# An NSA + HGRN2 decoder trunk on one core: the first HGRN projection pair, the order of the last two units, and where row-major weights lie

## The chip, the cores and the metric

The kernel runs on one of the eight cores of a Trainium2 chip. A core has TensorE (PE in the rows: matmuls; PEld: its weight loads), VectorE (DVE), ScalarE (ACT), GpSimd (POOL) and SyncE (SP), an on-chip memory of 128 partitions (SBUF), and a small accumulator memory that matmuls write (PSUM). Transfers between HBM and SBUF are DMAs; here SP issues those of weights and results, POOL those of the residual stream. The metric is the device time of one execution in microseconds (us), lower is better; several executions give a median.

## The reference, cut to what matters

The input is x, 512 tokens by 2048 features, float32. Two layers are computed, then a final RMSNorm:

```python
for layer in range(2):
    hn = rmsnorm(x, norm_w[layer])
    y = nsa_mixer(hn, ...) if layer == 0 else hgrn2_mixer(hn, ...)
    x = x + y
return rmsnorm(x, final_norm_w)
```

`nsa_mixer` is attention with compressed, selected and windowed keys over 16 heads of 128; its output is gated by silu(z) and projected by `w_out`. `hgrn2_mixer` is a gated linear recurrence:

```python
q, f, i, z = split(hn @ w_in)                   # 16 heads of 128 each
k = (1 - lb) * sigmoid(-f); q = silu(q)          # and the decay from f
o = recurrence over 512 tokens of (q, k, i, decay), per head
o = rmsnorm(o) * gnorm_w * silu(z); y = o @ w_out
```

So every HGRN head needs four projected inputs: F and Q (which give its decay, keys and queries), I (its values) and Z (its gate). All weights are float32 and are read once from HBM.

## The kernel before, in words

**Precision.** Each float32 operand is split into a rounded part `hi` (a ScalarE cast to fp32r) and the rest `lo` (a VectorE subtraction), `split`, L76 to L80. A product is three matmuls: hi·hi, hi·lo and lo·hi. The normalised stream lies in SBUF as `hhi` and `hlo`, 128 features by 512 tokens for each of 16 feature blocks (kt). Each weight load of 512 KB lands in a `raw` buffer and is split into two or four tiles `whi`/`wlo` of 512 floats per partition (tags `whi`, `wlo`, `ohi`, `olo`, four buffers each).

**NSA layer** (`nsa`, L649). Heads are worked in groups; at its end `out_proj_half` (L291) projects heads 12 to 15, tokens in two halves: first tiles 0 and 1, then tiles 2 and 3 of 128 tokens. After each half the sum x is written to a DRAM tile `xd` (POOL, L730) and `norm(1, t)` (L474) makes the new `hhi`/`hlo` of those tokens: square sums, a scale `xn` on ACT or DVE, four PE transposes for each 512 features, `y` on DVE, then the split. The pools of this layer have three raw buffers.

**HGRN layer** (`hgrn`, L912). It opens its own pools in the SBUF space that the NSA pools leave: level tiles (attT 2 x 2048 bytes, pick 3 x 512, masks 6 x 64 bytes per partition), a spacer `GAP` of 48 floats, then the weight tiles, work tiles and five raw buffers. In the NSA layer what lies in front of the weight tiles is causal, cmask, rt, kcmp, vcmp, gate and sw, 9,984 bytes. A tile of a new pool waits until the old tiles under it are done with.

The first unit there is head 0's F and Q, by `proj_pair` (L116): both weights are loaded and split whole, F into `whi`/`wlo`, Q into `ohi`/`olo`, and the tokens are taken in two halves of 256; each half is 48 matmuls for F and 48 for Q. All other F/Q pairs and the Z pairs go through `proj_product` (L168), which takes half of the contraction as seven products of 2 x 2 blocks (Strassen-like, over the sums `fm` made once by `forms`, L135) and the other half (`rest`) directly. A helper tile `s2` of 256 floats holds a partial sum. Its fifth product is the last reader of `fm` in a pair and stands between `rest(a)` and `rest(b)`.

I units go through `proj_rows` (L238): here the weights are the moving operand (256 columns, two heads at once) and `hhi`/`hlo` the stationary one, 192 matmuls for two heads. `hgrn_levels` computes from F and Q the within-chunk attention `attT`; `hgrn_inner` (L1099) needs `attT` and I; `hgrn_gate` needs Z.

**Order around the change.** The loop (L928) takes heads two at a time: levels of both, I of both, Z of both. While it runs, x lives in `xd`, and the SBUF place of x holds `fm`. The last two heads are written out: levels, I (L940), Z (L941), then `open_x` (L943) puts x back over `fm`, sixteen POOL loads of 256 KB (L947) fetch it, then `hgrn_inner` of both, the gates, `out_proj` of heads 12 and 13 (which adds to x in SBUF, L289) and `last_out_proj` of heads 14 and 15 (L510), whose four weight loads (L517) are split into the space of `hhi`/`hlo` blocks 0 to 7.

**Who sets the order.** The program order above is not the issue order: the framework simulates a time line while it builds, and interleaves instructions on each engine as they become ready there. On the chip each engine then runs its own list in order.

Of the kernel before, what the change touches and what calls it, by code (L numbers as in the profile page):

```python
# [52 lines left out]
class Trunk:  # L53
    def __init__(self, ctx, tc, aps):
        self.tc, self.nc, self.ctx = tc, tc.nc, ctx
        self.__dict__.update(aps)
        pool = lambda name, bufs, **k: ctx.enter_context(tc.tile_pool(name=name, bufs=bufs, **k))
        self.consts = pool("consts", 1)
        self.work = pool("work", 2)
        self.spill = pool("spill", 1, space=bass.MemoryType.DRAM).tile([S, D], F32, name="xd")  # L60
        self.pproj = pool("pproj", 2, space=PSUM)
        self.flip = 0
        self.ss = {}
        self.og, self.z = {}, {}
        self.spilled, self.atright = False, None


    def copy(self, out, in_):
# [15 lines left out]
        self.nc.sync.dma_start(raw, ap)  # L84
        return self.split_weights(raw, tags, share)

    def split_weights(self, raw, tags=("whi", "wlo"), share=False):

        _, nk, cols = raw.shape
        parts, step = [], 512 // cols  # L90
        for k0 in range(0, nk, step):
            n = min(step, nk - k0)
            hi, lo = (self.wpool.tile([128, n, cols], F32R, name=t, tag=t, bufs=4) for t in tags)
            self.split(raw[:, k0:k0 + n, :], hi, lo, share and k0)
            parts += [(hi[:, k, :], lo[:, k, :]) for k in range(n)]
        return parts
# [71 lines left out]
    def proj_product(self, w, ca, cb):  # L168


        nc = self.nc
        add = lambda o, a, b: nc.vector.tensor_tensor(out=o, in0=a, in1=b, op=ALU.add)
        raws = []
        for c0 in (ca, cb):
            raw = self.rawpool.tile([128, 2 * KP, 128], F32, name="raw", tag="raw")
            nc.sync.dma_start(raw, w[:2 * KP * 128, c0:c0 + 128].rearrange("(k p) n -> p k n", p=128))
            raws.append((raw[:, :KP], raw[:, KP:]))
        (b11, b21), (b12, b22) = raws

        def parts(src):  # L180
            hi, lo = (self.wpool.tile([128, KP, 128], F32R, name=t, tag=t, bufs=4) for t in ("whi", "wlo"))
            self.split(src, hi, lo)
            return hi, lo

        def product(dst, form, wts, start=False, stop=False):
            (hi, lo), (fhi, flo) = wts, self.fm[form]
            for k in range(KP):
                nc.tensor.matmul(dst, hi[:, k], fhi[:, k], start=start and k == 0, stop=False)
                nc.tensor.matmul(dst, hi[:, k], flo[:, k], start=False, stop=False)
                nc.tensor.matmul(dst, lo[:, k], fhi[:, k], start=False, stop=stop and k == KP - 1)  # L190

        def rest(acc, c0):
            src = w[2 * KP * 128:, c0:c0 + 128].rearrange("(k p) n -> p k n", p=128)
            for k, (hi, lo) in enumerate(self.load_split(src, [128, KT - 2 * KP, 128])):
                kt = 2 * KP + k
                for ts in (one, two):
                    stop = kt == KT - 1 and ts is two
                    nc.tensor.matmul(acc[:, ts], hi, self.hhi[:, kt, ts], start=False, stop=False)  # L198
                    nc.tensor.matmul(acc[:, ts], hi, self.hlo[:, kt, ts], start=False, stop=False)  # L199
                    nc.tensor.matmul(acc[:, ts], lo, self.hhi[:, kt, ts], start=False, stop=stop)  # L200

        one, two = slice(0, 256), slice(256, 512)
        a = self.pproj.tile([128, S], F32, name="acc", tag="acc")
        b = self.pproj.tile([128, S], F32, name="acc", tag="acc")
        d = self.pd.tile([128, S], F32, name="d", tag="d")
        sa, sb = (self.hp.tile([128, S], F32, name=n, tag=n, bufs=1) for n in ("sa", "sb"))
        s2 = self.hp.tile([128, 256], F32, name="s2", tag="s2", bufs=1)
        w2, w1 = parts(b21), parts(b11)
        product(a[:, one], 2, w2, start=True)
        product(d[:, two], 1, w1, start=True, stop=True)  # L210
        nc.scalar.copy(sa[:, one], d[:, two])
        t1, t3 = b11, b12
        add(t1, b11, b12)
        add(t3, b12, b22)
        w7 = parts(t3)
        product(d[:, one], 7, w7, start=True, stop=True)
        w3 = parts(b22)
        product(b[:, one], 3, w3, start=True)
        t2, t4 = b22, b21
        add(t2, t1, b22)  # L220
        add(t4, t2, b21)
        w4 = parts(t4)
        product(a[:, two], 4, w4)
        w6 = parts(t2)
        product(d[:, two], 6, w6, start=True, stop=True)
        add(s2, d[:, two], sa[:, one])
        add(sa[:, two], d[:, one], s2)
        rest(a, ca)
        add(sa, a, sa)
        w5 = parts(t1)  # L230
        product(d[:, two], 5, w5, start=True, stop=True)
        add(sb[:, one], d[:, two], s2)
        add(sb[:, two], d[:, one], sb[:, one])
        rest(b, cb)
        nc.vector.tensor_tensor(out=sb, in0=b, in1=sb, op=ALU.subtract)
        return sa, sb

    def proj_rows(self, w, c0, c1):  # L238
# [3 lines left out]
        for c in range(2):  # L242
            parts = []
            for r0 in range(c * 1024, (c + 1) * 1024, 512):
                raw = self.rawpool.tile([128, 4, 2, 128], F32, name="raw", tag="raw")
                if c1 == c0 + 128:
                    src = w[r0:r0 + 512, c0:c0 + 256].rearrange("(k p) (b n) -> p k b n", p=128, b=2)
                    self.nc.sync.dma_start(raw, src)
                else:
                    for b, cb in enumerate((c0, c1)):  # L250
                        self.nc.sync.dma_start(raw[:, :, b, :],
                                               w[r0:r0 + 512, cb:cb + 128].rearrange("(k p) n -> p k n", p=128))
                parts += self.split_weights(raw.rearrange("p k b n -> p k (b n)"))
            for i, acc in enumerate(accs):
                for k, (hi, lo) in enumerate(parts):
                    kt = c * 8 + k
                    first, last = kt == 0, kt == KT - 1
                    for t in range(2):
                        ts = slice((2 * i + t) * 128, (2 * i + t + 1) * 128)
                        self.nc.tensor.matmul(acc[:, t, :], self.hhi[:, kt, ts], hi, start=first and t == 0, stop=False)  # L260
                        self.nc.tensor.matmul(acc[:, t, :], self.hhi[:, kt, ts], lo, start=False, stop=False)  # L261
                        self.nc.tensor.matmul(acc[:, t, :], self.hlo[:, kt, ts], hi, start=False, stop=last and t == 1)  # L262
# [356 lines left out]
    def gates(self, w_in):  # L619
# [5 lines left out]
        for c in range(2):  # L625
            raw = self.rawpool.tile([128, 8, n], F32, name="raw", tag="raw")
            nc.sync.dma_start(raw, w_in[c * 1024:(c + 1) * 1024, NSA_GL:NSA_Z].rearrange("(k p) n -> p k n", p=128))
            for k0 in (0, 4):
                w = self.wpool.tile([128, 4, 128], F32R, name="whi", tag="whi", bufs=4)
                self.split(raw[:, k0:k0 + 4, :], w[:, :, :n], w[:, :, n:2 * n])  # L630
                for k in range(4):
                    kt = c * 8 + k0 + k
# [16 lines left out]
    def nsa(self):  # L649
# [28 lines left out]
        with ExitStack() as es:  # L678
# [48 lines left out]
            for tiles in ((0, 1), (2, 3)):  # L727
                self.out_proj_half(w_out, 12, last, tiles, self.square_sum)
                for t in tiles:
                    nc.gpsimd.dma_start(self.spill[t * 128:(t + 1) * 128, :], self.x_sb[t])  # L730
                    self.norm(1, t, pool=self.att)

    def query(self, w_in, h):

# [177 lines left out]
    def hgrn(self, out):  # L912
        nc, work, tc = self.nc, self.work, self.tc
        w_in, w_out = self.hgrn_w_in[0], self.hgrn_w_out[0]
        with ExitStack() as es:
# [5 lines left out]
            self.rawpool = es.enter_context(tc.tile_pool(name="raw5", reuse_waits="tile", bufs=5))  # L921
            self.ptr = es.enter_context(tc.tile_pool(name="ptr1", bufs=1, space=PSUM))
            self.pd = es.enter_context(tc.tile_pool(name="pd", bufs=1, space=PSUM))
            self.spilled = True
            self.plv = es.enter_context(tc.tile_pool(name="plv", bufs=2, space=PSUM))
            self.pst = es.enter_context(tc.tile_pool(name="pst", bufs=1, space=PSUM))
            self.pho = es.enter_context(tc.tile_pool(name="pho", bufs=1, space=PSUM))
# [9 lines left out]

            last = (N_HEADS - 2, N_HEADS - 1)
            levels = [self.hgrn_levels(w_in, h) for h in last]
            inputs = self.hgrn_inputs(w_in, last[0])  # L940
            self.z_pair(w_in, last[0])  # L941
            self.spilled = False
            self.open_x("xagain")  # L943
            for t in range(NT):
                for c in range(4):
                    cs = slice(c * 512, (c + 1) * 512)
                    nc.gpsimd.dma_start(self.x_sb[t][:, cs], self.spill[t * 128:(t + 1) * 128, cs])  # L947
            o = [self.hgrn_inner(h, *levels[i], inputs[:, :, i, :]) for i, h in enumerate(last)]
            for i, h in enumerate(last):
                self.hgrn_gate(w_in, w_out, h, o[i])  # L950
# [15 lines left out]
    def hgrn_levels(self, w_in, h):  # L966
# [4 lines left out]
        K = hp.tile([128, S], F32, name="K", tag="K")  # L971
        f = hp.tile([128, S], F32, name="f", tag="f", bufs=1)
        cf, cq = HG_F + h * 128, HG_Q + h * 128
        acc, accq = (self.proj_pair if h == 0 else self.proj_product)(w_in, cf, cq)
        nc.scalar.activation(f, acc, AF.Sigmoid)
        nc.scalar.activation(K, acc, AF.Sigmoid, scale=-1.0)
        nc.vector.tensor_scalar(f, f, oml, lb, op0=ALU.mult, op1=ALU.add)
# [209 lines left out]
```

## Time and profile before

| | us |
|---|---|
| median of 3 executions (range) | 2074.45 (2072.75 to 2076.51) |
| the profiled execution | 2072.67 |
| its span, first to last instruction | 2070.9 |
| PE busy in the span | 2012.1 (97%) |
| DVE busy | 1375.6 (66%) |
| ACT busy | 937.4 (45%) |
[...]

A matmul's recorded length holds its pipeline's depth, so neighbours overlap in the rows and a busy PE can still be slow; the distance between two starts is what a matmul costs. [...] In a row of the time line `x8` means eight instructions merged, and the bracket is the idle time before them and who ended it. All times are from one profiled execution.

### The profile page before, as it was taken

The numbers are of one execution on the slowest core, as the hardware profiler recorded it, in microseconds if no ns is written. First come the engines' busy times: TensorE is split into PE (matmuls) and PEld (weight loads), VectorE is DVE, ScalarE is ACT, GpSimd is POOL, SyncE is SP. The second block draws the span as 40 slices with busy tenths as digits, with TensorE's granted clock in tenths as the row PEclk, the third lists the DMA queues.
The fourth block names the chain that finished last, engine by engine and source line by source line (L and its number), as shares of the span: only waits on it lengthen the run. The fifth ranks groups of instructions, "written<-read, shape, count | busy, mean of one in ns | idle before, by whom it ended". The sixth has DMA issues, their size and how long they took to land.

```text
span 2070.9 us, 34906 instructions
## 1 busy us (share of the span) xinstructions
PE 2012.1 (97%) x13598; PEld 1834.8 (89%) x13598; DVE 1375.6 (66%) x3193; ACT 937.4 (45%) x1994; POOL 130.0 (6%) x131
## 2 busy tenths in 40 slices
PE   7999999999999999999799999999999999999987
PEld 7889889888988888889799999889998999989976
DVE  7634676566656565756887777567773777737866
ACT  5223564434444353446634353543534444444444
POOL 5000000000000000002200000110001100020033
PEclk9999999999999999999999999999999999999999
DMA  5344222323232322233432222562326613175242
GB/s 168 86 136 106 74 66 72 91 63 92 64 90 62 92 72 82 62 96 98 160 116 83 82 82 82 120 139 69 93 71 147 139 52 111 53 157 119 88 158 92
DMA packets 281462, 201.09 MB, mean 97 GB/s; under 512 B 9280, under 2 KB 255408, under 8 KB 280784
## 3 DMA queue, kind: packets, MB, share of 16 engines
q1 hardware_dynamic: 272528, 177.88, 29.6%
q0 software_dynamic: 8768, 20.98, 5.6%
q8 instruction: 107, 1.75, 0.3%
q14 instruction: 59, 0.48, 0.1%
HBM read 177.86 MB, written 20.97 MB: 96 GB/s over the span
## 4 chain that ended last, share of the span: by engine, by line
PE 67%; issue 25%; DVE 4%; POOL 2%; ACT 1%; DMA 1%; SPq 0%; DVEq 0%; POOLq 0%; ACTq 0%
PE acc L113 8%; PE acc L112 8%; PE acc L111 8%; PE acc L261 3%; PE acc L262 3%; PE acc L260 3%; PE acc L280 3%; PE acc L281 3%; PE acc L282 3%; PE acc L199 2%; PE acc L198 2%; PE acc L200 2%; PE pt L788 2%; POOL xd L286 2%; DVE hlo L80 1%
## 5 line engine op out<-in xcount | busy, mean ns | idle before, releaser
L80 DVE TENSOR_TENSOR wlo<-raw,whi 128x512 fp32r<-128x512 f32 x661 | 455.4, 701 | 347.8 <-ACT whi L78 343.2
L78 ACT CAST whi<-raw 128x512 fp32r<-128x512 f32 x681 | 411.3, 618 | 581.3 <-PE acc L112 187.5
L113 PE MATMUL acc<-hhi,wlo 128*128 128x512 f32 x736 | 288.7, 392 | 0.0
L112 PE MATMUL acc<-hlo,whi 128*128 128x512 f32 x736 | 288.3, 392 | 0.0
L111 PE MATMUL acc<-hhi,whi 128*128 128x512 f32 x736 | 288.1, 391 | 0.0
L261 PE MATMUL acc<-wlo,hhi 128*128 128x256 f32 x768 | 217.7, 283 | 0.0
L262 PE MATMUL acc<-whi,hlo 128*128 128x256 f32 x768 | 216.8, 282 | 0.0
L260 PE MATMUL acc<-whi,hhi 128*128 128x256 f32 x768 | 216.0, 281 | 0.0
L199 PE MATMUL acc<-hlo,whi 128*128 128x256 f32 x736 | 205.7, 279 | 0.0
L200 PE MATMUL acc<-hhi,wlo 128*128 128x256 f32 x736 | 205.3, 279 | 0.0
L198 PE MATMUL acc<-hhi,whi 128*128 128x256 f32 x736 | 205.2, 279 | 0.0
L281 PE MATMUL acc<-wlo,ohi 128*128 128x512 f32 x416 | 163.9, 394 | 0.0
L282 PE MATMUL acc<-whi,olo 128*128 128x512 f32 x416 | 163.2, 392 | 0.0
L113 PEld LDWEIGHTS acc<-hhi,wlo 128*128 128x128 f32 x736 | 138.3, 188 | 27.7
L280 PE MATMUL acc<-whi,ohi 128*128 128x512 f32 x416 | 160.3, 395 | 2.4 <-DVE x_all L289 2.4
L112 PEld LDWEIGHTS acc<-hlo,whi 128*128 128x128 f32 x736 | 138.3, 188 | 27.3
L111 PEld LDWEIGHTS acc<-hhi,whi 128*128 128x128 f32 x736 | 138.3, 188 | 27.2
L261 PEld LDWEIGHTS acc<-wlo,hhi 128*128 128x128 f32 x768 | 145.2, 189 | 0.8
L262 PEld LDWEIGHTS acc<-whi,hlo 128*128 128x128 f32 x768 | 145.2, 189 | 0.6
L260 PEld LDWEIGHTS acc<-whi,hhi 128*128 128x128 f32 x768 | 145.2, 189 | 0.2
L199 PEld LDWEIGHTS acc<-hlo,whi 128*128 128x128 f32 x736 | 138.7, 188 | 0.5
L200 PEld LDWEIGHTS acc<-hhi,wlo 128*128 128x128 f32 x736 | 138.7, 188 | 0.1
(322 smaller groups left out, 4486.4 us busy)
## 6 DMA issues: line engine op xcount, KB each, us to landing
raw<-in_hgrn_w_in_dram SPq DMA_DIRECT2D x128, 512.0 KB, 4.2
raw<-in_nsa_w_in_dram SPq DMA_DIRECT2D x96, 512.0 KB, 3.8
raw<-in_nsa_w_out_dram SPq DMA_DIRECT2D x40, 512.0 KB, 3.7
raw<-in_hgrn_w_out_dram SPq DMA_DIRECT2D x32, 512.0 KB, 4.0
xd<-yo POOLq DMA_DIRECT2D x48, 256.0 KB, 5.4
raw<-in_nsa_w_in_dram SPq DMA_DIRECT2D x32, 256.0 KB, 3.3
xd<-x_all POOLq DMA_DIRECT2D x4, 1024.0 KB, 5.3
x_all<-xd POOLq DMA_DIRECT2D x16, 256.0 KB, 6.8
```

Of the source, the lines that this page charges most:

```text
L78: self.nc.scalar.copy(hi, x)
L80: eng.tensor_tensor(out=lo, in0=x, in1=hi.bitcast(F32), op=ALU.subtract)
L111: self.nc.tensor.matmul(acc, hi, self.hhi[:, kt, :], start=first, stop=False)
L112: self.nc.tensor.matmul(acc, hi, self.hlo[:, kt, :], start=False, stop=False)
L113: self.nc.tensor.matmul(acc, lo, self.hhi[:, kt, :], start=False, stop=last)
L198: nc.tensor.matmul(acc[:, ts], hi, self.hhi[:, kt, ts], start=False, stop=False)
L199: nc.tensor.matmul(acc[:, ts], hi, self.hlo[:, kt, ts], start=False, stop=False)
L200: nc.tensor.matmul(acc[:, ts], lo, self.hhi[:, kt, ts], start=False, stop=stop)
L260: self.nc.tensor.matmul(acc[:, t, :], self.hhi[:, kt, ts], hi, start=first and t == 0, stop=False)
L261: self.nc.tensor.matmul(acc[:, t, :], self.hhi[:, kt, ts], lo, start=False, stop=False)
L262: self.nc.tensor.matmul(acc[:, t, :], self.hlo[:, kt, ts], hi, start=False, stop=last and t == 1)
L281: nc.tensor.matmul(acc, ohi, lo, start=False, stop=False)
```

## The change

Four edits, in the order in which the program meets them (`wpad` starts at 0).

1. Head 0's F/Q pair is no longer computed in `hgrn` but as the last statement of `nsa`, in the NSA layer's tiles and with its three raw buffers; `hgrn_levels(0)` picks up its two accumulators.
2. In the HGRN layer the `whi` and `wlo` buffers grow from 512 to 576 floats (256 bytes more each). The weights of `proj_rows` begin 32 floats (128 bytes) inside their buffer, all others at its start. In the NSA layer nothing is padded.
3. `s2` is no tile of its own any more but the second half of `sb`, which the product writes last.
4. For the last two heads Z comes before I: `z_pair` stays in front of `open_x` and the x loads, and I follows behind them.

```diff
+    def weight_part(self, tag, n=4, cols=128, rows=False):
+        pad = self.wpad if tag in ("whi", "wlo") else 0
+        off = 32 if pad and rows else 0
+        t = self.wpool.tile([128, 512 + pad], F32R, name=tag, tag=tag, bufs=4)
+        return t[:, off:off + n * cols].rearrange("p (k n) -> p k n", n=cols)
...
-            hi, lo = (self.wpool.tile([128, n, cols], F32R, name=t, tag=t, bufs=4) for t in tags)
+            hi, lo = (self.weight_part(t, n, cols, rows) for t in tags)
...
-            hi, lo = (self.wpool.tile([128, KP, 128], F32R, name=t, tag=t, bufs=4) for t in ("whi", "wlo"))
+            hi, lo = (self.weight_part(t, KP) for t in ("whi", "wlo"))
...
-        s2 = self.hp.tile([128, 256], F32, name="s2", tag="s2", bufs=1)
+        s2 = sb[:, two]
...
-                parts += self.split_weights(raw.rearrange("p k b n -> p k (b n)"))
+                parts += self.split_weights(raw.rearrange("p k b n -> p k (b n)"), rows=True)
...
                     nc.gpsimd.dma_start(self.spill[t * 128:(t + 1) * 128, :], self.x_sb[t])
                     self.norm(1, t, pool=self.att)
+            self.first = self.proj_pair(self.hgrn_w_in[0], HG_F, HG_Q)
...
-            self.spilled = True
+            self.spilled, self.wpad = True, 64
...
             levels = [self.hgrn_levels(w_in, h) for h in last]
-            inputs = self.hgrn_inputs(w_in, last[0])
             self.z_pair(w_in, last[0])
             self.spilled = False
             self.open_x("xagain")
...
+            inputs = self.hgrn_inputs(w_in, last[0])
             o = [self.hgrn_inner(h, *levels[i], inputs[:, :, i, :]) for i, h in enumerate(last)]
...
-        acc, accq = (self.proj_pair if h == 0 else self.proj_product)(w_in, cf, cq)
+        acc, accq = self.proj_product(w_in, cf, cq) if h else self.first
```

## Rows read from the trace of the kernel before

**Rows 1.** Windows: length; PE, PEld, DVE, ACT, POOL busy; granted clock, DMA share, GB/s.
```profile
1020.00:1036.00 16.00, 6.63 (x37) 4.76 (x35) 13.54 (x29) 9.97 (x20) 1.55 (x4) 0.88 0.54 196
1036.00:1042.00 6.00, 4.43 (x19) 4.14 (x20) 6.00 (x19) 3.97 (x8) 0.00 (x0) 0.50 0.58 175
...
1038.00:1062.00 24.00, 23.64 (x191) 23.64 (x192) 24.00 (x46) 11.02 (x15) 0.00 (x0) 0.91 0.36 104
1062.00:1085.00 23.00, 23.00 (x196) 22.91 (x195) 17.29 (x45) 6.55 (x12) 0.00 (x0) 1.00 0.40 115
...
2012.00:2015.00 3.00, 2.69 (x9) 2.44 (x10) 2.96 (x9) 0.27 (x1) 0.00 (x0) 0.50 0.60 189
```

**Rows 2.** Time line of PE between the layers: start, length, line, tiles [idle before].
```profile
1020.27 0.28 PE L307 MATMUL acc<-whi,olo 128*128 128x256 f32 x1
1023.90 1.09 PE L495 MATMUL pt<-ident,xn 128*128 128x128 f32 x8 [3.35 <-ACT xn L493]
...
1036.09 0.58 PE L130 MATMUL acc<-hhi,whi 128*128 128x256 f32 x1 [3.91 <-ACT whi L78]
...
1061.96 0.28 PE L260 MATMUL acc<-whi,hhi 128*128 128x256 f32 x1
```

**Rows 3.** Time line of ACT, between the layers and near the end.
```profile
1035.42 1.14 ACT L78 CAST whi<-raw 128x512 fp32r<-128x512 f32 x2 [0.90 <-DMA raw<-in_hgrn_w_in_dram]
...
2005.56 1.04 ACT L78 CAST hhi<-raw 128x1024 fp32r<-128x1024 f32 x1 [9.01 <-DMA raw<-in_hgrn_w_out_dram]
```

**Rows 4.** DVE from 1022 to 1038, by line: count, busy us, mean ns, idle before.
```profile
L80 DVE TENSOR_TENSOR hlo<-y,hhi 128x512 fp32r<-128x512 f32 x8 | 5.4, 680 | 0.0
L498 DVE TENSOR_TENSOR y<-pt,nw 128x512 f32<-128x512 f32 x8 | 5.4, 681 | 0.5 <-PE pt L495 0.5
L491 DVE TENSOR_SCALAR xn<-x_all,rs 128x512 f32<-128x512 f32 x4 | 1.8, 480 | 0.0
```

**Rows 5.** PE near the end: the last head's hgrn_inner.
```profile
2012.31 1.65 PE L1109 MATMUL sp<-I,KT 128*128 128x128 f32 x6 [9.42 <-DVE KT L74]
```

**Rows 6.** Time line of SP's queue at the same place.
```profile
1995.51 0.37 SPq L517 DMA_DIRECT2D raw<-in_hgrn_w_out_dram  x1
```

**Rows 7.** Time line of POOL there: the first and the last of the x loads.
```profile
1992.72 5.44 POOL L947 DMA_DIRECT2D x_all<-xd  x10 [120.06 <-PE d L190]
...
2006.01 0.55 POOL L947 DMA_DIRECT2D x_all<-xd  x1 [0.38 <-DMA x_all<-xd]
```

**Rows 8.** The page's DMA issues: count, KB each, median us from issue to landing.
```profile
raw<-in_hgrn_w_out_dram SPq DMA_DIRECT2D x32, 512.0 KB, 4.0
```

**Rows 9.** What PE waited for in all: us in total, times, longest.
```profile
PE acc L280 <- DVE x_all L289: 2.4, 3, 1.4
```

**Rows 10.** PE in proj_rows (three stretches), then proj_product: first and last of each.
```profile
346.74 0.28 PE L261 MATMUL acc<-wlo,hhi 128*128 128x256 f32 x1
...
352.98 0.28 PE L262 MATMUL acc<-whi,hlo 128*128 128x256 f32 x1
...
1062.75 0.28 PE L261 MATMUL acc<-wlo,hhi 128*128 128x256 f32 x1
...
1068.99 0.28 PE L262 MATMUL acc<-whi,hlo 128*128 128x256 f32 x1
...
1123.78 0.28 PE L199 MATMUL acc<-hlo,whi 128*128 128x256 f32 x1
...
1129.90 0.28 PE L199 MATMUL acc<-hlo,whi 128*128 128x256 f32 x1
...
1161.09 0.28 PE L261 MATMUL acc<-wlo,hhi 128*128 128x256 f32 x1
...
1165.80 0.28 PE L262 MATMUL acc<-whi,hlo 128*128 128x256 f32 x1
...
1206.43 0.28 PE L200 MATMUL acc<-hhi,wlo 128*128 128x256 f32 x1
...
1208.78 0.28 PE L189 MATMUL d<-fm,whi 128*128 128x256 f32 x1
```

More of the change, by code (lines that the diff above doesn't have):

```diff
@@ L64, in __init__ @@
         self.og, self.z = {}, {}
-        self.spilled, self.atright = False, None
+        self.spilled, self.atright, self.wpad = False, None, 0
     def copy(self, out, in_):
@@ L85, in load_split, with split_weights @@
         return self.split_weights(raw, tags, share)
-    def split_weights(self, raw, tags=("whi", "wlo"), share=False):
+    def weight_part(self, tag, n=4, cols=128, rows=False):
[3 more added lines that the diff above has]
+        return t[:, off:off + n * cols].rearrange("p (k n) -> p k n", n=cols)
+    def split_weights(self, raw, tags=("whi", "wlo"), share=False, rows=False):
         _, nk, cols = raw.shape
@@ L628, in gates @@
             for k0 in (0, 4):
-                w = self.wpool.tile([128, 4, 128], F32R, name="whi", tag="whi", bufs=4)
+                w = self.weight_part("whi")
                 self.split(raw[:, k0:k0 + 4, :], w[:, :, :n], w[:, :, n:2 * n])
```

## The prediction, made before the result was known

> **What bounds the kernel now.** I read the busy times first: PE is busy for nearly the whole span, so only two things can pay, stretches in which PE has nothing to run, and matmuls that cost more than they need. The windows by stage show where the first lie. There are two holes: between the layers PE is busy 6.63 of 16 us and then 4.43 of 6 us, and near the end there is one wait of 9.42 us [rows 1, 5]. Edits 1 and 4 stand exactly there. [...]
>
> The first hole is a chain. The last matmul of `out_proj_half` starts at 1020.27; then PE has only the transposes of `norm` for token tiles 2 and 3, paced by DVE, which is nearly full (13.54 of 16 us) [rows 1, 2, 4]. Only then do the weights of head 0's F arrive and get split (ACT waits for the DMA until 1035.42), and PE starts them at 1036.09 [rows 2, 3]. The pair of 192 matmuls gives way to I at 1061.96 [rows 2].
>
> The second hole is a queue. The x loads of 4 MB start when the Z pair's fifth product lets go of `fm` (1992.72) and the last is issued at 2006.01 [rows 7]. The weight load issued beside them at 1995.51 lands only when ACT's split of it starts, 2005.56: 10 us where the median of its kind is 4.0 [rows 3, 6, 8]. ACT runs its list in order, so the copies behind that split wait too, then DVE, then PE at 2012.31 [rows 3, 5]. [...]
>
> The sums below are made against the profiled execution, 2072.67 us; the median is 2074.45, 1.78 more.
>
> **Edit 1, the first pair inside the NSA layer.** It removes no work: 4 loads, 8 splits and 192 matmuls move. The tokens are taken in halves, and the first half (tiles 0 and 1) is normalised before the hole begins, so 96 of the 192 matmuls can run inside it. On SP the loads pass nothing but the last `w_out` loads and use the three NSA raw buffers. What limits the start is tiles: F's `whi`/`wlo` are free as the last out-projection steps finish, Q's `ohi`/`olo` hold heads 12 to 15 until the very last one, 1020.27. So most splits fall on DVE just when it is full.
>
> PE alone could do it by: 1020.55, plus 32 transposes at 1.09 us for eight [rows 2] = 4.4 at most, plus 192 matmuls. I take 0.120 us for each of these, not the 0.113 of the fast stretches, because in the NSA tiles proj_rows runs at 0.120 (6.24 us over 52 steps [rows 10]): 23.0. That is 1048.0, a gain of 14. DVE allows less. After 1020.6 it has one add into x (0.7), the norm's 12.6 us [rows 4], small operations of 0.6, and eight splits at 0.68 = 5.4: 1039.9 at the latest, some 1.3 less if two splits fit before 1020.6. The second half starts then, 1038.6, and lasts 96 x 0.120 = 11.5: 1050.1, a gain of 11.9. Late next is DVE: it is full from 1038 to 1062 (24.00 of 24) and has 5.7 us free in the 23 us after that [rows 1]. Brought forward by 12 us, with some 4 us of splits already done, it still has to do forms, masks and the splits of I: I take off 2. Edit 1: 10 us, between 5 (DVE's whole debt falls on PE) and 14.
>
> **Edit 4, Z before I at the end.** Again nothing is removed. `fm` is free one `rest(b)` (48 matmuls, 5.4 us at 0.113) and one I unit (192 x 0.1177 = 22.6 us) before the projections end, 28 us instead of 5. The x loads took from 1992.72 to some 2011 (the issue of 2006.01 plus the time of a load), 18 us, beside one weight load. So they are hidden with some 10 us to spare, and the L517 loads, which must wait for `hhi` blocks 0 to 7 and so for half of I, come after most of them. What goes: the 9.42, the later waits for x (at most 2.4) [rows 9], and 1.5 of the 3 us at the 1.2 GHz level [rows 1]: 13.3. What is late next: I is now last, so both `hgrn_inner` chains and gates hang on it. Their cover is `out_proj` of heads 12 and 13, 96 matmuls of 512 columns at about 0.227 = 21.8 us, which needs neither. I take 11.5, between 4 and 13.3.
>
> **Edit 2, where weights lie.** The table of starts gives a matmul of 256 columns, same type, clock 1.00 [rows 10]: NSA proj_rows 6.24 us over 52 steps = 0.120; HGRN proj_rows 6.24 over 55 = 0.1135 in one stretch and 4.71 over 40 = 0.1178 in another; proj_product 6.12 over 54 = 0.1133 and 2.35 over 20 = 0.1175. So one cost in NSA, and two in HGRN that both kinds of unit share and that last for a whole stretch. What differs between the layers is the tiles: before the weight tiles lie 9,984 bytes in NSA and 6,208 in HGRN, that is 0 and 64 bytes past a multiple of 256. My reading: the distance between the weight tile and `hhi`/`hlo` modulo 256 matters. With edit 2 the HGRN stationary weights keep theirs (buffers grow by 256), and proj_rows goes from +64 to +192; since its operands are the other way round than in proj_product, that is proj_product's own distance. There are 8 x 192 = 1536 such matmuls in HGRN. Bounds: all slow to all fast, 1536 x 0.0043 = -6.6 us; all fast to 0.120, 1536 x 0.0065 = +10. As both kinds show the same two costs I expect little: -1.
>
> [...]
>
> **Edit 3, `s2` in `sb`.** The same instructions. The new order to keep is that `sb`'s last reader (the next unit's activation) is done before `s2` is written, six products or 72 matmuls, 8.2 us, into the next pair: 0, at most a few tenths a pair.
>
> **Sum.** -10 - 11.5 - 1 = -22.5: 2072.67 - 22.5 = 2050.2, or 2052 as a median.
>
> **Rivals.**
> (a) The crowd only moves. If the last three I loads are issued beside the x loads, each costs 10 us instead of 4 and I starves: up to 9.4 of edit 4 comes back, about 2062. [...] Against: a Z raw buffer comes free at its last split, before `rest(a)`, so these loads are issued 48 or more matmuls (5 us) ahead of the x loads. 0.10.
> (b) DVE, not PE, sets the first stretch: splits placed between the norm's operations delay the norm, and the debt is carried on. Edit 1 gives about 0 to 2: about 2061. For it: DVE 24.00 of 24. Against: DVE is well below full in the loop. 0.08.
> (c) The other side: the longer buffers themselves put all HGRN weights at the NSA cost of 0.120. It decides if the distance that matters is one of more than 256 bytes, since buffers 2 and 4 now lie 256 off. Price: 4140 proj_product matmuls x 0.0045 (the mean of 0.0023 and 0.0067) = 18.6, proj_rows 1536 x 0.0044 = 6.8, and 672 of 512 columns with at most the same 0.0067 = 4.5: +30 against -21.5, so 2083, slower than before. Against: within a stretch, tiles 512 and 1024 bytes apart cost the same. 0.07.
> (d) The build's simulated order shuffles elsewhere and eats everything: about 2073. 0.06.
>
> **How the numbers follow.** Forecast 0.69, the rivals 0.31. Its own range is 2043 (14 + 13.3 and half of the 6.6 taken) to 2060; to leave out no more than 2 in 10 I take in (a) and (b): 2043 to 2065. A change of 0.2%, 4.1 us, is about what can be told from none: below 2070.3 fall the forecast, (a) and (b), 0.87 less a little for their tails: faster 0.86; same 0.06; slower 0.08.
>
> **What would show it.** Right: L130 matmuls starting before 1036 among the L495 transposes, at 1.00 clock; I's first matmul near 1050; POOL's x loads issued some 20 us before the last L262; no ACT wait of 9 us on a `w_out` load; proj_rows at 0.113 to 0.118. Wrong: DVE full and PE waiting on `wlo` after the norm; PE waiting on I's `whi` for a DMA; any HGRN stretch at 0.120.

## The result, and the profile after

| | before | changed |
|---|---|---|
| median (4 executions each), us | 2073.68 | 2059.79 |
| ratio, with its 95% interval | | 0.9933 (0.9916 to 0.9951) |
| the profiled execution, us | 2072.67 | 2060.98 |
| its span, us | 2070.9 | 2059.2 |
| PE busy in the span, us | 2012.1 | 2009.7 |
| mean granted clock of TensorE, share | 0.994 | 0.997 |

The change is 13.9 us faster by the medians; 22 were forecast (2052, range 2043 to 2065). Where the two profiled executions part can be read from the start of the same matmul in both traces. (The order in the loop is I of two heads, then Z of both, then F and Q of the next two: in both traces the unit behind the first I unit is the Z pair of heads 0 and 1, and not, as I wrote of the kernel before, all the levels of a pair of heads ahead of its I.)

```
first matmul of                          before     changed    lead
the first I unit                         1061.96    1052.32     9.6
Z of heads 0 and 1, the next unit        1087.6     1084.5      3.1
the second I unit                        1157.6     1153.4      4.2
the seventh I unit                       1767.0     1765.3      1.7
last_out_proj                            2038.9     2027.2     11.7
(the end of the span)                    2070.9     2059.2     11.7
```

So edit 1 brings 9.6 us to the first I unit and only 3 to 4 past it; 2.5 us are lost in the loop, where the instructions are the same; the end, edit 4, brings 10.0.

The windows of the changed kernel, with the columns and the first four stretches of [rows 1]:

```profile
1020.00:1036.00 16.00, 15.38 (x128) 14.74 (x126) 11.60 (x25) 10.54 (x21) 1.76 (x4) 1.00 0.58 212
1036.00:1042.00 6.00, 5.36 (x42) 4.93 (x42) 6.00 (x10) 1.84 (x3) 0.00 (x0) 1.00 0.00 0
1038.00:1062.00 24.00, 17.08 (x122) 16.39 (x122) 23.90 (x40) 10.75 (x15) 0.00 (x0) 0.86 0.24 71
1062.00:1085.00 23.00, 23.00 (x195) 22.92 (x195) 20.74 (x66) 6.61 (x13) 0.00 (x0) 1.00 0.39 111
```

The first hole is filled: PE is busy 15.38 of 16 us where it was 6.63, at a granted clock of 1.00. But a new hole stands in the third row, 17.08 of 24 us, and DVE is as full there as before. The time line of PE shows it:

```profile
1020.27 0.28 PE L137 MATMUL acc<-hhi,whi 128*128 128x256 f32 x1
...
1038.01 0.28 PE L139 MATMUL acc<-hhi,wlo 128*128 128x256 f32 x1
...
1049.03 0.28 PE L139 MATMUL acc<-hhi,olo 128*128 128x256 f32 x1
1052.32 0.38 PE L267 MATMUL acc<-whi,hhi 128*128 128x256 f32 x1 [3.00 <-ACT whi L78]
1055.51 0.58 PE L267 MATMUL acc<-whi,hhi 128*128 128x256 f32 x1 [2.81 <-DVE Q L988]
1057.19 0.58 PE L268 MATMUL acc<-wlo,hhi 128*128 128x256 f32 x1 [1.10 <-DVE wlo L80]
...
1060.56 0.41 PE L268 MATMUL acc<-wlo,hhi 128*128 128x256 f32 x1
```

The pair (L137 to L139 are now `proj_pair`) follows the out-projection without a gap and ends at 1049.31 (1049.03 + 0.28). Before, its last matmul began 0.12 us ahead of the 1061.96 of [rows 2] and so ended at 1062.12: 12.8 us are gained here. Then PE waits three times, 6.9 us, and from 1055.5 to 1061 the granted clock is 0.50: 17 steps, from 1057.19 to 1060.98, take 3.8 us, most of them 0.213 us each, where they would take 2.0 at 0.117 us, so 1.8 us more. (The clock records of this trace and of the one before hold only the shares 1.00 and 0.50, no frequency; what my forecasts call the 1.2 GHz level or stretch is the 0.50 of the traces.) With the waits taken out, the 192 matmuls of I took 25.1 us here and 22.5 before. What it waited for stands on ACT and DVE; first ACT, then DVE, in the same stretch:

```profile
1047.82 1.05 ACT L78 CAST fm<-raw 128x1024 fp32r<-128x1024 f32 x1 [2.44 <-DVE raw L150]
1048.89 1.28 ACT L983 ACT_TABLE_LOAD   x1
1050.18 0.60 ACT L983 ACTIVATE f<-acc 128x512 f32<-128x512 f32 x1
...
1051.16 0.60 ACT L987 ACTIVATE Q<-acc 128x512 f32<-128x512 f32 x1
1051.63 2.19 ACT L78 CAST whi<-raw 128x512 fp32r<-128x512 f32 x4
```

```profile
1050.52 1.22 DVE L80 TENSOR_TENSOR fm<-raw,fm 128x1024 fp32r<-128x1024 f32 x1
1051.65 1.22 DVE L150 TENSOR_TENSOR raw<-raw,hlo 128x1024 f32<-128x1024 f32 x1
...
1053.64 1.22 DVE L150 TENSOR_TENSOR raw<-raw,hlo 128x1024 f32<-128x1024 f32 x1
1054.78 0.68 DVE L988 TENSOR_TENSOR Q<-acc,Q 128x512 f32<-128x512 f32 x1
...
1056.46 1.28 DVE L80 TENSOR_TENSOR wlo<-raw,whi 128x512 fp32r<-128x512 f32 x2
```

`forms` (L150, and the splits into `fm`) and the masks stand ahead of everything that I needs. On ACT a split of `fm` waits for DVE, the sigmoids of F and Q follow, and I's first cast comes behind them, though its weights had landed at 1025.82. On DVE the read of Q's accumulator (there are two `acc` buffers, and I needs both) and I's first `wlo` come behind 1.2 us pieces of the forms.

At the end, the x loads on POOL and what PE waited for after 1960:

```profile
1961.92 5.48 POOL L954 DMA_DIRECT2D x_all<-xd  x10 [90.95 <-PE d L197]
...
1974.38 0.55 POOL L954 DMA_DIRECT2D x_all<-xd  x1 [0.50 <-DMA x_all<-xd]
```

```profile
PE acc L287 <- DVE x_all L296: 1.9, 2, 1.0
PE sp L1117 <- DVE I L74: 0.2, 1, 0.2
```

The loads are issued before and while I (1966.6 to 1995.2) runs, the 9.42 us wait of [rows 5] is gone, and 2.1 us of small waits are left.

### The profile page after: what moved, and what is told of

Read it like the earlier page. It is cut to its first block, busy times and chain, and to the rows that moved or that the text cites. A ratio compares the mean times of both kernels' runs of the same rounds, so it can differ in the third digit from the quotient of the medians.

```text
span 2059.2 us, 34901 instructions
## 1 busy us (share of the span) xinstructions
PE 2009.7 (98%) x13598; PEld 1832.0 (89%) x13598; DVE 1375.2 (67%) x3193; ACT 937.1 (46%) x1994; POOL 130.4 (6%) x131
## 4 chain that ended last, share of the span: by engine, by line
PE 67%; issue 25%; DVE 4%; POOL 2%; ACT 1%; DMA 1%; SPq 0%; DVEq 0%; POOLq 0%; ACTq 0%
PE acc L119 8%; PE acc L120 8%; PE acc L118 8%; PE acc L268 3%; PE acc L269 3%; PE acc L267 3%; PE acc L287 3%; PE acc L288 3%; PE acc L289 3%; PE acc L207 2%; PE acc L206 2%; PE acc L205 2%; PE pt L796 2%; POOL xd L293 2%; PE d L195 1%
```

## The experiments

Ratios are to the kernel before, with their 95% intervals. Traces are of one execution each.

**Each edit alone.** Edit 1 alone is:

```diff
+            self.first = self.proj_pair(self.hgrn_w_in[0], HG_F, HG_Q)   # last in nsa()
...
-        acc, accq = (self.proj_pair if h == 0 else self.proj_product)(w_in, cf, cq)
+        acc, accq = self.proj_product(w_in, cf, cq) if h else self.first
```

> The kernel before with edit 1 alone. Theory A (my reading of the two traces): the pair itself ends some 12.7 us sooner, at about 1049.3, but the first I unit then waits for its weights and runs its first matmuls at the 1.2 GHz level, so that about 3 us are left where the next pair begins: 2.5 to 4.5 us faster than before, near 2070, with PE waits of 6 to 7 us in all around I's first matmuls. Theory B: the stall belongs to the longer weight buffers, which lie over more of the NSA layer's tiles and so come free later: without edit 2 most of the 10 us that I forecast is there, near 2064.

Measured: 2070.89 beside 2074.62, ratio 0.9983 (0.9974 to 0.9991): 3.7 us faster. Its trace has the same three waits, 3.0, 2.6 and 1.1 us, with the weight buffers at their old length. Theory A holds, B falls.

> The kernel before with edit 3 alone. Theory A: the same instructions, no wait that costs: within 1 us of before. Theory B: the loss of about 2 us over the HGRN loop (three waits of PE after out_proj grew from 3.7 to 5.6 us together) comes from sb being held longer: 1 to 2 us slower than before, with the wait of PE at the first product behind out_proj at 1.5 to 2.1 us instead of 1.2.

Measured: 2076.10, ratio 1.0003 (0.9994 to 1.0012). No difference that can be told; the waits behind out_proj were 1.71, 1.36 and 1.37 us, between the two theories.

Edits 2 and 3 together:

> The kernel before with edits 2 and 3 (edit 2 does not fit without the room that edit 3 makes). Theory A: proj_rows costs some 0.6 ns less a matmul over 1536, proj_product about the same: between -1 and 0 us. Theory B: the loss of about 2 us over the loop comes with the longer buffers: 1 to 2.5 us slower than before, with longer waits of PE behind out_proj.

Measured: 2075.73, ratio 1.0003 (0.9994 to 1.0011). Nothing that can be told from none, and no loss of 2 us.

Edit 4 alone:

```diff
-            inputs = self.hgrn_inputs(w_in, last[0])
             self.z_pair(w_in, last[0])
...                                                       # open_x and the x loads
+            inputs = self.hgrn_inputs(w_in, last[0])
```

> The kernel before with edit 4 alone. Theory A: the whole 9.4 us wait near the end goes and nearly all of the 1.2 GHz stretch behind it: 10 to 12 us faster than before, near 2062, no PE wait over 1.5 us after 1960. Theory B: part of the gain of the end in the changed kernel hangs on the other edits (weights landing earlier): under 8 us.

Measured: 2064.11, ratio 0.9951 (0.9938 to 0.9963): 10.5 us faster; the longest PE wait near the end was 1.0 us. Theory A. The three groups alone add up to -3.7 + 1.1 - 10.5 = -13.1, the whole change measured -13.9: no sign beyond the noise that the edits touch one another.

**Why the first I unit starves.** All of the following start from the changed kernel.

```diff
                     levels = self.hgrn_levels(w_in, i)
-                    if i == 0:
-                        self.forms()
                     if i == h:
                         inputs = self.hgrn_inputs(w_in, h)
+                    if i == 0:
+                        self.forms()
```

> The changed kernel with the forms of head 0 behind the first I unit in the program instead of before it. Theory D (I's three waits, 3.0 + 2.8 + 1.1 us, come from the order on DVE and ACT: the forms' additions and splits stand ahead of I's splits and of the read of Q's accumulator): the waits at 1049 to 1057 go, I begins within 1 us of the pair's end, no 1.2 GHz stretch follows: 5 to 9 us faster than the changed kernel, if the forms are still ready for the next pair. Theory P (I's weight tiles lie where the pair's tiles lie, and can't be written before the pair's last matmuls): the first wait of 3.0 us stays as it is, and the gain is at most 4. Theory F: the forms come too late now and PE waits for fm instead at about 1080: no gain or a loss.

Measured: 2057.90, ratio 0.9920 (0.9905 to 0.9934), 2 us under the changed kernel, with overlapping intervals. What PE waited for between 1040 and 1150, and two windows:

```profile
PE acc L268 <- DVE wlo L80: 1.9, 2, 1.1
PE acc L267 <- ACT whi L78: 1.2, 1, 1.2
PE d L195 <- ACT whi L78: 1.0, 1, 1.0
PE acc L197 <- DVE wlo L80: 0.2, 1, 0.2
```

```profile
1038.00:1062.00 24.00, 22.05 (x171) 21.53 (x170) 21.87 (x51) 10.21 (x16) 0.00 (x0) 0.93 0.25 81
1062.00:1085.00 23.00, 20.90 (x172) 20.14 (x172) 23.00 (x53) 8.23 (x14) 0.00 (x0) 1.00 0.40 116
```

The next unit begins at 1077.3, 7.2 us sooner than in the changed kernel, and of I's 6.9 us of waits 3.1 remain. The order was thus most of what starved I, though the 5 to 9 us of theory D were not gained. Of the first wait of 3.0 us only 1.2 remain, so theory P explains 1.2 at most (I's cast still stands directly behind the sigmoid of Q, which waits for the pair's last matmul; whether the place of the tiles put it there stays open). But 2.3 of the 7.2 us are only work put off: 19 of the 24 small matmuls of head 0's levels that ran among I's now run behind them. DVE is now full for the second window, the next unit waits 1.2 us (for its weights' splits, not for `fm` as theory F had it), and the products up to the second I unit cost 120.9 ns on average instead of 117.2 (118.8 in a second trace of the changed kernel). At the second I unit (1152.2) only 1.2 us of the 7.2 are left: the no gain of theory F, by other waits. The debt moves.

```diff
-        f5, f6, f3, f7 = (self.rawpool.tile(..., name="raw", tag="raw") for i in range(4))
+        f5, f6 = (self.rawpool.tile(..., name="raw", tag="raw") for i in range(2))
+        f3, f7 = (self.hp.tile([128, KP, 256], F32, name="I", tag="I") for i in range(2))
```

> The changed kernel with two of the forms' four temporaries in the (still unused) two buffers of I instead of raw buffers. Theory R (three of I's four weight loads are issued late, at 1046.7, 1051.8 and 1057.8, since the forms hold four of the five raw buffers, and this is what starves I): the loads go by 1030 and 5 to 9 us come back. Theory D: the loads go early too, but the first splits stay behind the forms on DVE and ACT: the waits before 1057 stay within 1.5 us of the 6.9, gain 0 to 2.

Measured: 2058.71, ratio 0.9919 (0.9904 to 0.9934). Three of I's loads are now issued by 1024.4, and PE's waits, 5.6 us in all, are still of the same three kinds:

```profile
PE acc L268 <- ACT whi L78: 3.0, 1, 3.0
PE acc L268 <- DVE Q L989: 1.5, 1, 1.5
PE acc L269 <- DVE wlo L80: 1.1, 1, 1.1
```

The second I unit begins at 1154.3 (1153.4 in the changed kernel). Theory R falls: two more loads that were issued early bring back 1.3 us of the 6.9 us of waits, and nothing by the second I unit.

Next, the masks on GpSimd (`nc.vector` to `nc.gpsimd` in `level_masks`, all but three operations on bits).

> The changed kernel with the comparisons, products and copies that build the level masks on GpSimd instead of DVE (some 4 to 5 us of DVE between 1050 and 1066). Theory D: what stands ahead of I's first wlo on DVE gets 2 us shorter: PE waits about 5 us instead of 6.9 and 1.5 to 3 us are gained. Theory P or R: within 1 us of the changed kernel.

Measured: 2058.53, ratio 0.9919 (0.9902 to 0.9935); PE waited 6.1 us, and the second I unit begins at 1155.0. D's 1.5 to 3 us aren't there in the trace, and the 1.3 by the medians are not told from none. DVE, the same additions and multiplications in the changed kernel and then in this one (count, busy us, mean ns):

```profile
L1035 DVE TENSOR_TENSOR Q<-Q,f 128x256 f32<-128x256 f32 x1 | 0.4, 411 | 0.0
L1041 DVE TENSOR_TENSOR tot<-f 128x256 f32<-128x256 f32 x1 | 0.4, 415 | 0.0
L985 DVE TENSOR_SCALAR f<-f,oml,lb 128x512 f32<-128x512 f32 x1 | 0.5, 537 | 0.0
```

```profile
L1035 DVE TENSOR_TENSOR Q<-Q,f 128x256 f32<-128x256 f32 x1 | 0.7, 656 | 0.0
L1041 DVE TENSOR_TENSOR tot<-f 128x256 f32<-128x256 f32 x1 | 0.7, 676 | 0.0
L985 DVE TENSOR_SCALAR f<-f,oml,lb 128x512 f32<-128x512 f32 x1 | 0.5, 534 | 0.0
```

With GpSimd at work beside it, many DVE operations of two SBUF tensors take up to 0.27 us longer, but not all: of those with 128x256 elements between 1059 and 1073 us, the five of L1035 and L1041 grow and that of L1015 stays at 0.41. L985, which reads a single tensor, keeps its length.

So the masks were taken off this stretch without GpSimd:

```diff
+            self.early_masks(cpool)     # in nsa(), after lower_bounds: build on DVE, store to DRAM
...
-            self.level_masks()          # in hgrn_levels(0)
+            nc.gpsimd.dma_start(self.allpick, self.kept[0])
+            nc.gpsimd.dma_start(self.allmask, self.kept[1])
```

> The changed kernel with the level masks built on DVE early in the NSA layer, kept in DRAM and fetched by two DMAs of GpSimd where they were built before. Theory D2 (between 1038 and 1085 the sum of DVE's work is the bound, and GpSimd's help gave nothing because DVE's own operations got longer beside it): some 5 us of DVE work are gone, PE's waits around I's first matmuls fall from 6.9 to under 5 us, DVE's operations keep their length, 2 to 5 us faster than the changed kernel, near 2056. Theory O (only the order on DVE and ACT matters, its sum does not): within 1 us of the changed kernel.

Measured: 2056.92, ratio 0.9910 (0.9897 to 0.9924). The waits fell from 6.9 to 5.4 us, but the next unit begins at 1084.1 (1084.5) and the second I unit at 1153.6 (1153.4): in the trace nothing is gained here, as theory O has it. DVE stayed full in the first window, and what the shorter waits gave went to the clock: 26 of I's steps instead of 17 fell in the stretch at 0.50. The 2.9 us by the medians lie in D2's range, but the intervals overlap.

```profile
1038.00:1062.00 24.00, 18.59 (x128) 17.90 (x128) 23.90 (x31) 10.75 (x15) 0.00 (x0) 0.86 0.30 88
```

> The same with the forms behind the first I unit. Theory D2: with the forms behind I the debt fell on the next pair (PE waits of 1.1 and 1.0 us, and all but 1.2 us of the 7.2 us gained at I's end were lost by the second I unit); 5 us less of DVE work there are kept as PE time: 4 to 7 us faster than the changed kernel, near 2054. Theory O: as the kernel with the forms behind I alone, near 2058.

Measured: 2053.13, ratio 0.9889 (0.9876 to 0.9903): 22.3 us faster than before (2075.47 beside it), and clear of the changed kernel's interval. PE's waits between 1040 and 1150, and the windows:

```profile
PE acc L267 <- ACT whi L78: 1.2, 1, 1.2
PE acc L268 <- DVE wlo L80: 0.6, 2, 0.4
PE d L195 <- ACT sa L218: 0.2, 1, 0.2
```

```profile
1038.00:1062.00 24.00, 22.39 (x185) 21.86 (x184) 20.77 (x34) 10.67 (x17) 0.00 (x0) 1.00 0.25 83
1062.00:1085.00 23.00, 22.56 (x189) 22.17 (x188) 22.36 (x40) 10.05 (x17) 0.00 (x0) 1.00 0.40 115
```

The second I unit begins at 1147.8, 5.6 us sooner than in the changed kernel and 4.4 sooner than with the forms behind I alone: D2's 4 to 7 us are there, O's 2058 isn't. The four traces side by side, in us, with the matmuls of I as distances of starts less PE's idle time (22.5 us before the change):

```
                              changed  forms behind I  masks early    both
PE's wait ahead of I              3.0             1.2          3.0     1.2
PE's waits inside I               3.9             1.9          2.4     0.6
I's 192 matmuls without waits    25.1            24.4         26.2    23.3
level matmuls among them           24               5           24      16
start of the next unit         1084.5          1077.3       1084.1  1076.3
start of the second I unit     1153.4          1152.2       1153.6  1147.8
```

In the traces either half by itself gains little and both together do, in part because only there the clock stays up (1.00 in both windows): the order decides whom DVE's debt hits, the sum how much of it hits PE. By the medians the halves gave 1.9 and 2.9 us and both 6.7; that this is more than their sum is clearer in the traces, of which there is one each. In a second trace of the changed kernel the second I unit begins at 1154.8, so these starts scatter by 1.4 us at least. This version beats both kernels.

**Where weights lie.**

```diff
-        off = 32 if pad and rows else 0
+        off = 0
```

> The changed kernel with the longer weight buffers, but the weights of proj_rows at the start of their buffer, as all others. My reading (the distance to hhi and hlo modulo 256 sets what a matmul costs; the buffers' growth by 256 bytes doesn't change it): proj_rows in HGRN goes back from a mean of 116.2 to 116.8 or 116.9 ns, as before the change, 1 us slower than the changed kernel. Rival (the spacing of the buffers is what moved proj_rows): it stays at 116.2.

Measured: 2058.69, ratio 0.9920 (0.9906 to 0.9933): no difference that can be told. From all starts of proj_rows in HGRN that follow one another by less than 0.125 us, the mean distance is 117.0 ns (1390 of them), against 116.2 in the changed kernel and 116.9 before. All the traces fall in the same two groups: 115.94 to 116.32 in the nine with the offset, 116.85 to 117.05 in the five without. The offset, not the buffers' growth, moves it, and it is worth 1536 x 0.8 ns = 1.2 us.

```diff
+            shift = es.enter_context(tc.tile_pool(name="shift", bufs=1)).tile([128, 16], F32, name="shift")
             t.wpool = es.enter_context(tc.tile_pool(name="weights", bufs=4))
```

> The changed kernel with all weight, raw and attention tiles of the NSA layer 64 bytes further on. My reading of the three costs of a matmul (the distance of the weight tile to hhi and hlo modulo 256 sets them): NSA's proj_rows, out_proj_half and the first pair go from 0.120 to 0.1134 or 0.1177 us each, 1344 matmuls, 3 to 9 us faster than the changed kernel, if the 512-column matmuls of proj stay at 0.2268. Rival: the cost is not one of place (or of a larger distance): NSA's proj_rows stay at 0.120 and the time within 1 us.

Measured: 2067.45, ratio 0.9960 (0.9946 to 0.9975): about 7.5 us slower than the changed kernel, where 3 to 9 faster were expected. First and last start of four undisturbed stretches: proj_rows (128 steps), proj (95 steps), out_proj_half (18 steps), the first pair (70 steps), and under it proj in the changed kernel (95 steps):

```profile
344.94 0.28 PE L267 MATMUL acc<-whi,hhi 128*128 128x256 f32 x1
...
360.02 0.28 PE L269 MATMUL acc<-whi,hlo 128*128 128x256 f32 x1
...
364.02 0.40 PE L118 MATMUL acc<-hhi,whi 128*128 128x512 f32 x1
...
386.19 0.40 PE L120 MATMUL acc<-hhi,wlo 128*128 128x512 f32 x1
...
1008.73 0.28 PE L313 MATMUL acc<-wlo,ohi 128*128 128x256 f32 x1
...
1010.89 0.28 PE L313 MATMUL acc<-wlo,ohi 128*128 128x256 f32 x1
...
1029.88 0.29 PE L137 MATMUL acc<-hhi,whi 128*128 128x256 f32 x1
...
1037.83 0.28 PE L138 MATMUL acc<-hlo,ohi 128*128 128x256 f32 x1
```

```profile
360.55 0.40 PE L118 MATMUL acc<-hhi,whi 128*128 128x512 f32 x1
...
382.11 0.39 PE L120 MATMUL acc<-hhi,wlo 128*128 128x512 f32 x1
```

Proj_rows go from 0.120 to 0.1178 us, the pair from 0.120 (11.02 us over 92 steps from 1038.01) to 0.1136, as the reading has it. But `proj`, 2208 matmuls of 512 columns, goes from 0.2269 to 0.2334 in this stretch, which the reading didn't have, and that loses more than the others gain. `out_proj_half` stays at 0.120, against what I expected, and this says what kind of place matters: its two operands (`whi`/`wlo` and `ohi`/`olo`) both moved by 64 bytes, while in the other three kinds one moved and `hhi`/`hlo` stayed. So in these runs it is the place of the two operands relative to one another; that it counts modulo 256 is not shown beyond the buffers' growth by 256 bytes, which changed nothing. Place sets the price here, and one place is not good for all: these 64 bytes took the pair from 0.120 to 0.1136 us and `proj` from 0.2269 to 0.2334.

**The loss in the loop.**

> The changed kernel itself once more. From the second I unit to the seventh the traces so far took 608.8 to 611.9 us with the same instructions, the changed kernel's own the longest, 2.5 us above before's 609.4. Theory L: this differs by the execution (how long the loads behind out_proj take, and at which of its two costs a stretch of matmuls runs): another profile of the same kernel lies elsewhere in 608.5 to 612, and more runs bring the median to 2058 to 2060. Rival: the 2.5 us are the change's own (the longer buffers or s2 together with the other order): 611 to 613 again, median 2060 or more.

Measured: 2060.15, ratio 0.9925 (0.9911 to 0.9938). From the second to the seventh I unit this profile took 610.0 us (611.9 in the first); its waits behind out_proj were 1.39, 1.11 and 1.40 us (2.13, 1.53 and 1.90). The kernel with edit 4 alone, whose loop is that of the kernel before, took 611.3 where before took 609.4. Theory L: the 2.5 us lost in the loop belonged for the most part to that execution, not to the change. The median, just above L's 2058 to 2060, doesn't speak for it.

## Why the prediction was right and wrong

Right, in sign and range; too much gain by 8 us, and nearly all of that in edit 1. The total lies at the very end of the forecast's own range (2060), and it does so by luck in part: edit 1 fell below its own lower bound, and edit 4 came out near its forecast. Step by step:

- **Edit 1, the pair itself: right.** Forecast: second half from 1038.6, end at 1050.1, matmuls at 0.120. Measured: 1038.0, 1049.31, 0.120.
- **Edit 1, what is late next: wrong, and this is the step that failed.** "Late next is DVE: it is full from 1038 to 1062 (24.00 of 24) and has 5.7 us free in the 23 us after that. [...] I take off 2." DVE was rightly named and its debt far too small: of the 12.8 us at the pair's end 3.1 were left at the next pair, so 9.7 came off, not 2: 6.9 us of waits and 2.6 us more for I's own matmuls, 1.8 of it in the stretch at a granted clock of 0.50. I had weighed DVE's work as a sum and gave the clock no term here. But DVE runs its list in order, and the list put forms and masks ahead of I's splits: the first `wlo` began at 1056.46, 4.1 us after PE had begun with its `whi` (1052.32). So PE stood still for the sake of sums that were not due until 1084. Both parts are shown: the order alone brings back 1.2 us at the second I unit, 5 us less work on DVE alone nothing in the trace, both together 5.6 there and 6.7 by the medians. The 1.2 us of wait ahead of I that stay in that kernel are open. The sign that I had named for it was seen: DVE full (23.90 of 24) and PE waiting on `wlo`. The gain, 3.7 us alone, lies even below the 5 that I gave as the lower bound. It is near rival (b) in size, by half of its mechanism: the norm was not delayed (its last transposes ended at 1037.8), the debt was carried on.
- **Edit 4: right.** 11.5 forecast, 10.0 by the traces, 10.5 alone. The wait of 9.42 us went, the stretch at a granted clock of 0.50 behind it too (1.00 from 1960 to 2045), 2.1 us of small waits stayed. No run shows the 1.2 GHz in the sum's term of 1.5 us; from 2012 to 2015 the windows show 0.50 before [rows 1] and 1.00 after. Rival (a) did not come true: the last of I's loads was issued by 1954.1, 8 us ahead of the x loads, as the text against it had it. The crowd did move: two `w_out` loads issued beside the x loads, at 1964.89 and 1968.88, took 10.2 and 11.0 us to land, where the median of their kind in this trace is 3.8. But out_proj, which needs them, begins only at 1995.8.
- **Edit 2: right, and its reading shown in part.** -1 forecast; -1.0 to -1.3 by the distances between starts, nothing that the medians can tell. That the place of the operands relative to one another moves the price is shown by the 64 bytes in the NSA layer: where the weight tiles moved and `hhi`/`hlo` stayed, a 512-column step went from 0.2269 to 0.2334 us, and in `out_proj_half`, where both operands moved, a step stayed at 0.120. What picks between the two prices in HGRN, 0.1135 and 0.1178, stays open: with every tile in its place, two traces of the changed kernel had 41% and 52% of the steps of proj_product above 0.1155. Rival (c), all HGRN weights at 0.120, did not come true.
- **Edit 3: right**, 0 forecast, no difference that can be told.
- **The loop:** I gave it no term; its 2.5 us in the first trace are mostly one execution's.

## What to carry to other kernels

When work is pulled forward into a hole, ask of each engine not only whether its sum fits but what stands ahead of the next needed instruction in its list; here a full DVE turned 12.8 us of early start into 3.1 one unit later. Take work off that stretch and change its order together: here either alone mostly moved the debt. Read a matmul's price from the distance of starts, since where its operands lie moved it here by 2 to 5% (0.120 to 0.1178 and 0.1136 us, 0.2269 to 0.2334), and try a shift on the kind that runs most often.

## What the runs showed that I had not expected

GpSimd's help is paid back by DVE: with it at work, five DVE operations on two SBUF tensors of 128x256 went from between 0.41 and 0.42 us to between 0.66 and 0.68. And 64 bytes have opposite signs for two kinds of matmul in one layer: of the matmuls with one operand moved, those of 256 columns gained 2 to 5% (0.120 to 0.1178 and 0.1136 us) and those of 512 columns lost 3% (0.2269 to 0.2334), while those with both operands moved kept their price (0.120).
